# The state-space layer's GELU moved from the mix phase into the state-space units, and norms and bias rows issued sooner, in a hybrid state-space and attention block

## The chip, the cores and the metric

The kernel runs on one core of a Trainium2 chip. The metric is the time of one execution on the device in microseconds (us), and the median of several runs. Engines are named as in the profile: PE is TensorE (matmuls; PEld its weight loads), DVE is VectorE, ACT is ScalarE, POOL is GpSimd, SP is the engine whose queue issues nearly all DMA transfers (SPq).

## The reference

One layer over 2048 positions with model width 1024, all in 32-bit floats:

```python
proj = rmsnorm(x, norm_mix_g) @ w_in              # u (512), q, k, v (512 each)
# head group A: 32 groups of 16 channels, 64 complex states per group
_, states = lax.associative_scan(combine, (a, bu), axis=1)
y = einsum(states, c).real + d_skip * u
y = jax.nn.gelu(y)                                # the tanh form
y_ssm = y * jax.nn.sigmoid(y @ w_glu + b_glu)
# head group B: each 64-row chunk attends to itself and the 8 chunks before
probs = softmax(q k / 8 + relative_bias)
y_att = probs @ v                                 # 8 heads of 64
x = x + concat(rmsnorm(y_ssm), rmsnorm(y_att)) @ w_out
h2 = rmsnorm(x)
x = x + (silu(h2 @ w_gate) * (h2 @ w_up)) @ w_down
return rmsnorm(x)
```

## The kernel before

Products of 32-bit floats are made of three matmuls: each operand is split into a rounded high part (a cast on ScalarE) and a rest (a subtraction on VectorE), `split` at L153; names ending in h and l, or hi and lo, are such pairs.

The phases in order: a prologue (to about 145 us) with the state-space matrices and the state-space input u; the attention phase (to about 700 us); the mix phase (to about 960 us), which makes the GLU, the two norms and the output projection; gate and up; down.

The attention phase walks 128 steps, one for each query block of 512 rows (sb, four), head pair (pr), head (hh) and quarter (qp) of 128 queries. In a step `scores` makes the products of queries and keys (sc), adds the bias rows and takes the minimum in one VectorE instruction (mn<-sc,nba or nbb, L866), and ScalarE takes the exponential (L869). Two steps later `transp` transposes the row on TensorE (pt), and ScalarE and VectorE split it (pth L884, ptl L885). After a head's four steps `pv_head` multiplies by v (pj). The bias rows of a head are loaded by `load_nb` into one of two buffers (nba, nbb) while the head before is in work.

Beside the steps run generators called units. A `Unit` has a first and a last step, and at each step its generator goes on as far as its share asks; `pre` lets its first part, mostly loads, go earlier. `hT_unit` loads rows of x for the next query block (xt, raw), norms them (L744) and splits them (hi L745, lo L746). `qk_unit` and `v_unit` make the projections (pf). The state-space layer is eight blocks b of four groups: `ssm_front` loads U and multiplies by Bst, then scans on GpSimd; `ssm_back` multiplies by Tm and Vm, copies the result over U (L652) and stores it to the array y in memory (L654). Odd blocks and block 0 share one buffer U, the other even blocks the buffer rsn; X holds a block's states, XG the states shifted by one.

The tables SX and SY give the steps at which a block's front and back start; HTA and HTS those of the hT units, counted from the query block's first step. TensorE's instructions stay in the order in which the code emits them. Those of the other engines are ordered by a scheduler that goes by its own estimate of when operands and buffers are ready, so an instruction may stand far from its place in the code. Each engine then runs its queue strictly in order.

At step 119 (OPEN) the mix phase's first part becomes one more unit. `fetch` reads y back from memory into yr: for each partition 4 x 8 x 128 elements, in which neighbours in position stand 128 elements apart. `load` applies the GELU to yr with a gathering pattern into contiguous ys (L1050) and splits ys into gh and gl. `glu` multiplies by the GLU weights (wgh, wgl, whose raw rows come through two buffers sg) and multiplies ys by the sigmoid. For the first two blocks of 512 positions (late) the biased product goes into yr (L1077), one sigmoid covers all four quarters (L1079), and the products ys follow (L1081). Sums of squares (sq) give the norm's scale by Newton steps on VectorE (L98 to L110).

## Time and profile before

| | |
|---|---|
| median of 3 runs | 2264.99 us (2262.37 to 2267.28) |
| profiled execution: its own time | 2267.91 us |
| its span, mean granted TensorE clock | 2266.1 us, 0.982 |
| TensorE busy | 2165.6 us, 96% |
| VectorE, ScalarE, GpSimd busy | 1542.4, 1003.3, 351.2 us |
| TensorE busy in 650 to 700 and 700 to 750 us | 33.70 and 41.19 of 50 us |

The profile is one execution, so durations and gaps come from it, and its own time is what a sum of them is held against. In the rows of a timeline the first number is the start, the second the busy time, and the bracket at the end says how long the engine stood idle just before and which instruction ended it.

### The profile page before, as it was taken

What the parts mean: (1) busy time and instruction counts of PE and PEld (TensorE: products, weight loads), DVE (VectorE), ACT (ScalarE), POOL (GpSimd) and SP (SyncE); (2) the same over time, 40 slices, a digit from 0 to 9 for tenths busy, and PEclk for the clock granted to TensorE, in tenths of its full rate; (3) what the DMA queues carried; (4) which work ended last, traced back from release to release, by engine and by line L of the source; (5) the groups of instructions that cost most, each with busy time, mean ns of one, the idle gap of its engine ahead of it and who ended that gap; (6) DMA issues with size and microseconds to landing.
All of it is one profiled execution on the core that took longest, in us unless ns stands there. A gap on an engine that the chain in (4) does not pass through costs nothing.

```text
span 2266.1 us, 30134 instructions
## 1 busy us (share of the span) xinstructions
PE 2165.6 (96%) x10632; PEld 1825.8 (81%) x10632; DVE 1542.4 (68%) x2695; ACT 1003.3 (44%) x1656; POOL 351.2 (15%) x827
## 2 busy tenths in 40 slices
PE   8988899999997899999999999999999999999997
PEld 6777788898986788778888887888888778888886
DVE  7756666556557756776766668766656477688776
ACT  5445555556557442353333335333333443353322
POOL 2246576656500000000000000000000010000000
PEclk9999999999998899999999999999999999999999
DMA  8878876666552435754556457645433395465652
GB/s 276 254 244 261 268 233 207 192 190 205 187 168 100 138 109 188 251 168 144 180 176 209 162 198 269 199 163 190 140 97 112 102 385 182 167 227 181 216 183 75
DMA packets 194903, 430.41 MB, mean 190 GB/s; under 512 B 19904, under 2 KB 38384, under 8 KB 187648
## 3 DMA queue, kind: packets, MB, share of 16 engines
q1 hardware_dynamic: 187104, 403.58, 53.8%
q0 software_dynamic: 7648, 24.92, 3.6%
q8 instruction: 83, 1.36, 0.2%
q14 instruction: 68, 0.56, 0.1%
HBM read 288.95 MB, written 131.10 MB: 185 GB/s over the span
## 4 chain that ended last, share of the span: by engine, by line
PE 78%; DMA 7%; DVE 6%; ACT 3%; issue 2%; SPq 0%; DVEq 0%; ACTq 0%
PE X L76 20%; PE ps L76 17%; PE Y L76 10%; PE pf L76 10%; PE big L76 6%; PE W L76 5%; PE pj L76 4%; PE pt L79 2%; PE sc L76 2%; DMA acc<-x 2%; DMA lo<-hc 1%; DMA xt<-in_xt 1%; DVE lo L153 1%; DMA hc<-gh 1%; DVE ptl L885 1%
## 5 line engine op out<-in xcount | busy, mean ns | idle before, releaser
L76 PE MATMUL X<-hi,c 128*128 128x512 f32 x1408 | 450.8, 391 | 7.4 <-DVE c L153 5.1
L76 PE MATMUL ps<-hd,hd 128*128 128x512 f32 (+1 forms) x1968 | 429.6, 380 | 3.0 <-DVE hd L153 2.0
L76 PEld LDWEIGHTS ps<-hd,hd 128*128 128x128 f32 x1968 | 357.5, 189 | 73.6 <-DVE hd L153 2.7
L76 PEld LDWEIGHTS X<-hi,c 128*128 128x128 f32 x1408 | 265.1, 188 | 64.1 <-DVE c L153 6.0
L76 PE MATMUL X<-lo,c 128*128 128x512 f32 x704 | 274.6, 390 | 0.0
L153 ACT CAST hd<-hd 128x1536 fp32r<-128x1536 f32 (+1 forms) x106 | 147.5, 1394 | 232.5 <-DMA hd<-hq 170.9
L76 PE MATMUL Y<-hi,c 128*128 128x512 f32 x704 | 226.0, 392 | 3.8 <-DVE c L153 2.3
L153 DVE TENSOR_TENSOR hd<-hd 128x1536 fp32r<-128x1536 f32 (+1 forms) x106 | 174.1, 1644 | 36.2 <-ACT hd L153 35.8
L153 DVE TENSOR_TENSOR c<-S,c 128x512 fp32r<-128x512 f32 x176 | 121.0, 688 | 103.6 <-ACT c L153 103.3
L1516 POOL DMA_DIRECT2D hd<-hq x7 | 5.3, 755 | 1173.2 <-PE X L76 1161.5
L1408 ACT COPY u<-X 128x512 f32<-128x512 f32 x132 | 77.4, 587 | 199.9 <-PE X L76 199.9
L153 ACT CAST c<-S 128x512 fp32r<-128x512 f32 x176 | 109.5, 622 | 122.5 <-PE Y L76 63.8
L76 PE MATMUL big<-m,woh 128*128 128x512 f32 x512 | 162.6, 399 | 0.0
L76 PEld LDWEIGHTS Y<-hi,c 128*128 128x128 f32 x704 | 133.3, 189 | 32.4 <-DVE c L153 2.8
L1550 DVE TENSOR_TENSOR acc<-acc,ps 128x512 f32<-128x512 f32 x196 | 130.2, 682 | 41.6 <-PE ps L76 41.3
L76 PEld LDWEIGHTS X<-lo,c 128*128 128x128 f32 x704 | 132.6, 188 | 27.4
L76 PE MATMUL pf<-hi,w 128*128 128x512 f32 x416 | 149.1, 410 | 0.0
L153 ACT CAST c<-raw 128x512 fp32r<-128x512 f32 x132 | 82.2, 622 | 149.1 <-PE Y L76 69.1
L76 PE MATMUL Y<-lo,c 128*128 128x512 f32 x352 | 137.7, 391 | 0.0
L885 DVE TENSOR_TENSOR ptl<-pt,pth 128x640 fp32r<-128x640 f32 (+3 forms) x152 | 98.3, 647 | 56.1 <-ACT pth L884 54.7
L869 ACT ACTIVATE s<-s,mn 128x640 f32<-128x640 f32 (+4 forms) x128 | 98.0, 765 | 64.1 <-DVE mn L866 58.1
L884 ACT CAST pth<-pt 128x640 fp32r<-128x640 f32 (+3 forms) x152 | 83.8, 551 | 85.6 <-PE pt L79 80.9
(448 smaller groups left out, 4274.1 us busy)
## 6 DMA issues: line engine op xcount, KB each, us to landing
w<-wss SPq DMA_DIRECT2D x36, 1024.0 KB, 6.2
hq<-g SPq DMA_DIRECT2D x140, 256.0 KB, 2.1
hd<-hq SPq DMA_DIRECT2D x35, 768.0 KB, 4.4
hd<-wc SPq DMA_DIRECT2D x35, 768.0 KB, 6.0
raw<-in_w_gate SPq DMA_DIRECT2D x44, 512.0 KB, 3.7
raw<-in_w_up SPq DMA_DIRECT2D x44, 512.0 KB, 4.2
wc<-px SPq DMA_DIRECT2D x66, 256.0 KB, 3.1
wss<-w SPq DMA_DIRECT2D x12, 1024.0 KB, 6.5
```

The source lines that it names most:

```text
L76: return self.tc.keep_in_program_order(self.tc.nc.tensor.matmul(*a, **b))
L79: return self.tc.keep_in_program_order(self.tc.nc.tensor.transpose(*a, **b))
L153: return nc.scalar.copy(hi, raw), nc.vector.tensor_tensor(lo, raw, f32(hi), op=ALU.subtract)
L869: nc.scalar.activation(s[:, :nk], s[:, :nk], AF.Exp, bias=mn[:], scale=-1.0, accum_out=sums[sb, pr][:, hh, qp : qp + 1])
L884: nc.scalar.copy(pth[:, a:b, qp, :], pt[:, a:b, :])
L885: nc.vector.tensor_tensor(ptl[:, a:b, qp, :], pt[:, a:b, :], f32(pth[:, a:b, qp, :]), op=ALU.subtract)
L1408: nc.scalar.copy(u[:], ps[:])
L1516: (nc.gpsimd if aside else nc.sync).dma_start(f32(lo), src.rearrange("g p c -> p g c"))
L1550: V.tensor_tensor(a, a, ps[:], op=ALU.add)
```

## The change

The GELU is taken out of the mix phase. In `ssm_back` it is made by hand from half the result, u: Square and Tanh on ScalarE, two instructions on VectorE, with XG as the room for the intermediate; 0.5 goes into the copy, and the store to y, still one transfer for the block, comes two yields after the last product. `ssm_back` now spans five steps instead of two, and the fronts and backs of blocks 5 to 7 start one to three steps earlier. `glu` and `load` read yr directly, with the gathering pattern in the splits gh and gl and in the products ys; the late bias and sigmoid now work on contiguous ys. `hT_unit`'s second part is cut in two, norms first and splits later, and its loads and norms come four or more steps earlier; the bias rows are loaded at the second quarter of the head before instead of the third.

```diff
QS = 4, 5, 6, 7, 0, 1, 2, 3
-HTA = -12, -9
+HTA = -16, -13
 HTS = -8, -6
-HTP = 2
+HTN = -13, -8
 PRO = 0, 0, 2, 2, 2, 2, 0, 0, 0
...
 MAGIC = 12582912.0
+GELU = 0.044715
 F2 = NF // 2
...
         k.XG = k.t(p, "XG", [P, GB, NC])
-        nc.gpsimd.memset(k.XG[:, :, 0:1], 0.0)
     XG = k.XG
+    nc.gpsimd.memset(XG[:, :, 0:1], 0.0)
     XGv = XG[:].rearrange("p (q g) c -> p q g c", g=2)
...
             k.ta.matmul(ps[:, g2, :], vm[:, g, :], XG[:, g, :], start=False, stop=True)
-        nc.scalar.copy(U[:, 2 * q : 2 * q + 2, :], ps[:])
+        u, t = U[:, 2 * q : 2 * q + 2, :], XG[:, 2 * q : 2 * q + 2, :]
+        nc.scalar.activation(u, ps[:], AF.Copy, scale=0.5)
+        nc.scalar.activation(t, u, AF.Square)
         yield
+    for q in range(GP):
+        u, t = U[:, 2 * q : 2 * q + 2, :], XG[:, 2 * q : 2 * q + 2, :]
+        nc.vector.scalar_tensor_tensor(t, t, 0.25 / GELU, u, op0=ALU.add, op1=ALU.mult)
+        nc.scalar.activation(t, t, AF.Tanh, scale=8.0 * GELU * math.sqrt(2.0 / math.pi))
+        yield
+    for q in range(GP):
+        u, t = U[:, 2 * q : 2 * q + 2, :], XG[:, 2 * q : 2 * q + 2, :]
+        nc.vector.scalar_tensor_tensor(u, t, 1.0, u, op0=ALU.add, op1=ALU.mult)
+        yield
+    yield
+    yield
     nc.sync.dma_start(S["y"].rearrange("j (c g) t -> (j c) (g t)", c=CH)[:, GB * NC * b : GB * NC * (b + 1)], U.rearrange("p g t -> p (g t)"))
...
 SSM_F = 1 + GP + 7 + 7 + 3 + 4 + 1
-SSM_B = 1 + GP + 1
+SSM_B = 1 + 3 * GP + 3
 ST = 2, 10
-SX = 4, 24, 35, 48, 61, 74, 87, 100
-SY = 20, 36, 49, 62, 75, 88, 101, 114
+SX = 4, 24, 35, 48, 61, 73, 85, 97
+SY = 20, 36, 49, 62, 75, 87, 99, 111
...
+            def norm(q):
+                nc.vector.scalar_tensor_tensor(xts[q], xts[q], k.gm[:, q : q + 1], S["rsn"][:, ts], op0=ALU.mult, op1=ALU.mult)
+
...
                     load(q, 2)
+                for q in range(q0, q1):
+                    yield
+                    norm(q)
             for q in range(q0, q1):
                 yield
-                if q0 == 0 and q + 2 < q1:
-                    load(q + 2)
-                xt = xts[q]
+                if q0 == 0:
+                    if q + 2 < q1:
+                        load(q + 2)
+                    norm(q)
                 for v, n in zip(hT[sb], ("hi", "lo")):
                     v.append(k.t(aw, f"{n}{q}x" if q < DB and sb % 2 else f"{n}{q}", [P, SB], F32R)[:])
-                nc.vector.scalar_tensor_tensor(xt, xt, k.gm[:, q : q + 1], S["rsn"][:, ts], op0=ALU.mult, op1=ALU.mult)
-                nc.scalar.copy(hi[q], xt)
-                nc.vector.tensor_tensor(lo[q], xt, f32(hi[q]), op=ALU.subtract)
+                nc.scalar.copy(hi[q], xts[q])
+                nc.vector.tensor_tensor(lo[q], xts[q], f32(hi[q]), op=ALU.subtract)
             yield
...
             hd = st_head[sb, h]
-            if qp == 2 and (sb, h) < (NSB - 1, H - 1):
+            if qp == 1 and (sb, h) < (NSB - 1, H - 1):
                 nbs[(h + 1) % H] = load_nb((h + 1) % H)
...
         psum2 = cx.enter_context(tc.tile_pool(name="aps2", bufs=1, space=bass.MemoryType.PSUM, reuse_waits="tile"))
+        hts = {sb: hT_unit(sb, DB) for sb in range(1, NSB)}
         units = []
...
                     units.append(Unit(hT_unit(sb, 0, DB), 2 + DB, g0 + HTA[0], g0 + HTA[1], 2))
-                units += [Unit(hT_unit(sb, DB), 2 + KT - DB, g0 + HTS[0], g0 + HTS[1], HTP), Unit(qk_unit(sb, 0), QK_N, g0 + C[0], g0 + C[1], 3, light=LIGHT)]
+                units += [Unit(islice(hts[sb], 1 + KT - DB), 1 + KT - DB, g0 + HTN[0], g0 + HTN[1], 1), Unit(hts[sb], 1 + KT - DB, g0 + HTS[0], g0 + HTS[1]), Unit(qk_unit(sb, 0), QK_N, g0 + C[0], g0 + C[1], 3, light=LIGHT)]
             units.append(Unit(v_unit(sb, 0), V_N, g0 + C[1], g0 + C[2], 2, light=LIGHT) if sb else Unit(v0, V_N, *V0, done=1))
...
         for b in range(NG // GB):
-            units.append(Unit(ssm_front(k, sp, psum, S, b, k.ssm_eng), SSM_F, SX[b], SX[b] + 9, SX[b] - 2 if b == 0 else 2 if b == 1 else 5, light=SL))
-            units.append(Unit(ssm_back(k, sp, psum, S, b), SSM_B, SY[b], SY[b] + 2, 6, light=SL))
+            units.append(Unit(ssm_front(k, sp, psum, S, b, k.ssm_eng), SSM_F, SX[b], SX[b] + 9, SX[b] - 2 if b == 0 else 2 if b == 1 else 3, light=SL))
+            units.append(Unit(ssm_back(k, sp, psum, S, b), SSM_B, SY[b], SY[b] + 5, 6, light=SL))
         N = len(steps)
...
-        def load(sb, one=False):
+        def byt(a):
+            return a.rearrange("p (c j) -> p c j", j=L)
+
+        def load(sb):
             b = B()
             b.o = {}
-            yt = k.t(my, "ys", [P, 4, SB], bufs=2)
-            b.ys, b.g = [yt[:, f] for f in range(4)], []
+            b.yt = k.t(my, "ys", [P, 4, SB], bufs=2)
+            b.ys, b.g = [b.yt[:, f] for f in range(4)], []
             if sb and sb % 2 == 0:
                 fetch(sb)
-            yv = b.yr = yrs[0][:, :, :, (sb % 2) * 64 : (sb % 2 + 1) * 64]
-            fs = [slice(0, 4)] if one else [slice(f, f + 1) for f in range(4)]
-            for s in fs:
-                nc.scalar.activation(yt[:, s].rearrange("p f (c j) -> p f c j", j=L), yv[:, s].rearrange("p f j c -> p f c j"), AF.Gelu_apprx_tanh)
+            b.yr = yrs[0][:, :, :, (sb % 2) * 64 : (sb % 2 + 1) * 64].rearrange("p f j c -> p f c j")
             for f in range(4):
                 gh, gl = k.t(my, f"gh{f}", [P, SB], F32R), k.t(my, f"gl{f}", [P, SB], F32R)
-                split(k, gh[:], gl[:], b.ys[f])
+                split(k, byt(gh[:]), byt(gl[:]), b.yr[:, f])
                 b.g.append((gh, gl))
...
-
-            def by8(a):
-                return a.rearrange("p (a b) -> p a b", a=L)
...
                 if late:
-                    nc.vector.tensor_scalar(b.yr[:, f], by8(ps[:, :512]), bg[:, f : f + 1], None, op0=ALU.add)
+                    nc.vector.tensor_scalar(b.ys[f], ps[:, :512], bg[:, f : f + 1], None, op0=ALU.add)
                     if f == 3:
-                        nc.scalar.activation(b.yr, b.yr, AF.Sigmoid)
+                        nc.scalar.activation(b.yt[:], b.yt[:], AF.Sigmoid)
                         for i in range(4):
-                            nc.vector.tensor_tensor(by8(b.ys[i]), by8(b.ys[i]), b.yr[:, i], op=ALU.mult)
+                            nc.vector.tensor_tensor(byt(b.ys[i]), byt(b.ys[i]), b.yr[:, i], op=ALU.mult)
                 else:
...
                     nc.scalar.activation(sg[:], ps[:, :512], AF.Sigmoid, bias=bg[:, f : f + 1])
-                    nc.vector.tensor_tensor(b.ys[f], b.ys[f], sg[:], op=ALU.mult)
+                    nc.vector.tensor_tensor(byt(b.ys[f]), byt(sg[:]), b.yr[:, f], op=ALU.mult)
                 yield
...
         wr = rx.enter_context(tc.tile_pool(name="wr", reuse_waits="tile", bufs=2, side="right"))
-        b = load(0, True)
+        b = load(0)
         load_a(b, 0)
...
             yield
-        nxt = load(1, True)
+        nxt = load(1)
         for _ in range(PZ):
```

Three places where instructions stand otherwise; line numbers of the changed kernel are some 1 to 20 higher for the same operation.

ScalarE at the start of the mix phase: L869 (L889 after) is the exponential, s the softmax row, wgh a GLU weight's high part. Before:

```order
L869 ACTIVATE s_7962,sm_7946<-s_7962,mn_7963 128x640
L869 ACTIVATE s_7982,sm_7946<-s_7982,mn_7983 128x640
L1050 ACT_TABLE_LOAD
L1050 ACTIVATE ys_8026<-yr_7910 128x2048
L153 CAST wgh_1710_7915<-sg_7917 128x512
L153 CAST wgh_1713_7921<-sg_7923 128x512
L908 COPY yt_8007<-pj_7990 64x512
L884 CAST pth_8010<-pt_8012 128x5x128
L153 CAST gh_1742_8028<-ys_8026 128x512
L153 CAST gh_1744_8032<-ys_8026 128x512
L153 CAST gh_1746_8036<-ys_8026 128x512
```

After:

```order
L154 CAST gh_1742_8098<-yr_7981 128x512
L889 ACTIVATE s_8035,sm_8017<-s_8035,mn_8036 128x640
L904 CAST pth_7928<-pt_8039 128x5x128
L154 CAST gh_1744_8102<-yr_7981 128x512
L889 ACTIVATE s_8053,sm_8017<-s_8053,mn_8054 128x640
L154 CAST gh_1746_8106<-yr_7981 128x512
L154 CAST gh_1748_8110<-yr_7981 128x512
L154 CAST wgh_1710_7986<-sg_7988 128x512
L154 CAST wgh_1713_7992<-sg_7994 128x512
L928 COPY yt_8078<-pj_8061 64x512
L904 CAST pth_8081<-pt_8083 128x5x128
L1044 ACTIVATE sq_8122<-ya_1750_8114 128x512
```

Then one more cast wgh and the next exponential follow. The load of tables and the Gelu are gone, and the casts gh read yr and stand between exponentials.

SP's queue at the end of block 0: y<-U stores the block, U<-u reloads the buffer for block 1, xt and raw are rows for `hT_unit`, k<-ks loads keys. Before:

```order
L654 DMA y_65<-U_1708 128x1024
L788 DMA q2h_2507<-q2h_2507 64x512
L789 DMA q2l_2508<-q2l_2508 64x512
L788 DMA q2h_2510<-q2h_2510 64x512
L789 DMA q2l_2511<-q2l_2511 64x512
L711 DMA w_2618<-wss_74 128x2048
L726 DMA xt_2659<-in_xt 128x512
L726 DMA raw_2661<-in_xt 128x2x512
L726 DMA raw_2663<-in_xt 128x2x512
L566 DMA U_2665<-u_64 128x1024
L566 DMA Bst_2667<-bsts_70 128x512
```

After:

```order
L731 DMA wss_74<-w_2452 128x2048
L567 DMA Bst_2678<-bsts_70 128x512
L780 DMA k_597_2746<-ks_68 128x512
L668 DMA y_65<-U_1708 128x1024
L814 DMA ks_68<-k_547_2532 128x512
L814 DMA ks_68<-k_550_2535 128x512
L550 DMA nbb_1550<-nbs_69 64x576
L567 DMA U_2676<-u_64 128x1024
L551 DMA nbb_1550<-nbs_69 64x576
```

The rows of xt and raw now stand ahead of these; the store stands four places before the reload instead of nine, behind a load of k.

VectorE near the first query block's end, 640 columns a step from here on. L744 (L745 after) is the norm of a row of x, ptl the rest of the softmax split. Before:

```order
L866 ISA s_3269,mn_3270<-sc_3264,nba_107 128x640
L866 ISA mn_3270 128x1
L744 SCALAR_TENSOR_TENSOR raw_4423<-raw_4423,g_mix_87,rsn_93 128x512
L909 TENSOR_TENSOR ya_3024<-pj_3277,yt_3286 64x512
L744 SCALAR_TENSOR_TENSOR raw_4423<-raw_4423,g_mix_87,rsn_93 128x512
L885 TENSOR_TENSOR ptl_3290<-pt_3291,pth_3289 128x5x128
L744 SCALAR_TENSOR_TENSOR raw_4425<-raw_4425,g_mix_87,rsn_93 128x512
L866 ISA s_3322,mn_3323<-sc_3317,nba_107 128x640
L866 ISA mn_3323 128x1
L918 TENSOR_TENSOR ya_3024<-ya_3024,pj_3326 128x512
L744 SCALAR_TENSOR_TENSOR raw_4425<-raw_4425,g_mix_87,rsn_93 128x512
```

After, the norms of the same rows stand among the last steps of the query block before:

```order
L745 SCALAR_TENSOR_TENSOR raw_4221<-raw_4221,g_mix_87,rsn_93 128x512
L905 TENSOR_TENSOR ptl_2857<-pt_2944,pth_2856 128x2x128
L745 SCALAR_TENSOR_TENSOR raw_4223<-raw_4223,g_mix_87,rsn_93 128x512
L886 ISA s_2988,mn_2989<-sc_2985,nbb_1550 128x256
L886 ISA mn_2989 128x1
L905 TENSOR_TENSOR ptl_2857<-pt_2992,pth_2856 128x128
L745 SCALAR_TENSOR_TENSOR raw_4223<-raw_4223,g_mix_87,rsn_93 128x512
L905 TENSOR_TENSOR ptl_2857<-pt_2992,pth_2856 128x3x128
L886 ISA s_3028,mn_3029<-sc_3025,nbb_1550 128x384
L886 ISA mn_3029 128x1
```

And at the place where they stood:

```order
L886 ISA s_3168,mn_3169<-sc_3163,nba_107 128x640
L886 ISA mn_3169 128x1
L905 TENSOR_TENSOR ptl_3046<-pt_3173,pth_3045 128x128
L745 SCALAR_TENSOR_TENSOR xt_4048<-xt_4048,g_mix_87,rsn_93 128x512
L905 TENSOR_TENSOR ptl_3046<-pt_3173,pth_3045 128x2x128
L745 SCALAR_TENSOR_TENSOR xt_4219<-xt_4219,g_mix_87,rsn_93 128x512
L847 TENSOR_TENSOR v_676_3053<-pf_3181,v_676_3053 128x4x64
L886 ISA s_3233,mn_3234<-sc_3228,nba_107 128x640
L886 ISA mn_3234 128x1
L905 TENSOR_TENSOR ptl_3046<-pt_3237,pth_3045 128x128
```

The four norms of raw have moved ahead by more than 20 rows, and one or two of xt are left in their place.

## The prediction

> **What bounds the kernel now.** I read the page first, then TensorE's waits, then a table of stretches, and only then single instructions. The page's first part:
>
> ```profile
> PE 2165.6 (96%) x10632; PEld 1825.8 (81%) x10632; DVE 1542.4 (68%) x2695; ACT 1003.3 (44%) x1656; POOL 351.2 (15%) x827
> ```
>
> TensorE is busy for 96% of the span, and nothing in this change adds or removes a matmul. So the change moves the time only where TensorE stands still, and the question is how much of that standing still it touches. The table of stretches (columns: bounds, length, then busy time of TensorE, weight load, VectorE, ScalarE and GpSimd, TensorE's granted clock, DMA share, GB/s) says where it is:
>
> ```profile
> 450.00:650.00 200.00, 199.68 (x1270) 183.03 (x1269) 111.90 (x203) 115.16 (x230) 107.38 (x268) 1.00 0.61 186
> 650.00:700.00 50.00, 33.70 (x184) 28.68 (x183) 28.08 (x50) 36.74 (x53) 0.00 (x0) 0.86 0.53 163
> 700.00:750.00 50.00, 41.19 (x201) 33.58 (x201) 45.12 (x90) 35.56 (x50) 0.00 (x0) 0.90 0.41 134
> ```
>
> From 450 to 650 us, the later attention steps, TensorE never stops. From 650 to 750, where attention ends and the mix phase begins, it stands for 25.1 us of 100, and the granted clock falls to 0.86 and 0.90. Its waits say for whom it stands; first from 640 to 760 us, then in the earlier attention steps, 150 to 430 us (columns: us in total, times, longest):
>
> ```profile
> PE pt L79 <- DVE ptl L885: 13.8, 3, 6.4
> PE big L79 <- DVE no L110: 7.9, 1, 7.9
> ```
>
> ```profile
> PE pt L79 <- DVE ptl L885: 8.0, 7, 3.1
> PE sc L76 <- DVE mn L866: 5.8, 1, 5.8
> PE sc L76 <- DVE k L792: 4.1, 1, 4.1
> ```
>
> **Part 1: the GELU leaves the mix start.** The 13.8 us are three gaps in the last softmax steps. TensorE's next transposes (pt) wait for ptl, which waits for the cast pth; behind them the exponentials stand in ScalarE's queue. ScalarE's timeline shows what lies between two exponentials:
>
> ```profile
> 675.15 1.28 ACT L1050 ACT_TABLE_LOAD   x1 [0.30 <-DMA yr<-y]
> 676.45 3.69 ACT L1050 ACTIVATE ys<-yr 128x2048 f32<-128x2048 f32 x1
> ...
> 684.47 0.61 ACT L153 CAST wgh<-sg 128x512 fp32r<-128x512 f32 x1
> ...
> 686.67 1.28 ACT L869 ACT_TABLE_LOAD   x1
> 687.97 0.83 ACT L869 ACTIVATE s<-s,mn 128x640 f32<-128x640 f32 x1
> ...
> 691.33 1.28 ACT L1050 ACT_TABLE_LOAD   x1
> 692.62 3.80 ACT L1050 ACTIVATE ys<-yr 128x2048 f32<-128x2048 f32 x1
> ```
>
> Out go two Gelus (3.69 + 3.80 = 7.5 us) and these three loads of tables (3 x 1.28 = 3.8 us): 11.3 us. Some is paid back, since the casts gh now read the stored rows through a stride. What a stride costs is in these groups (busy us, mean ns):
>
> ```profile
> L1050 ACT ACTIVATE ys<-yr 128x512 f32<-128x512 f32 x8 | 8.7, 1124 | 2.3 <-DVE m L153 2.3
> ...
> L153 ACT CAST gh<-ys 128x512 fp32r<-128x512 f32 x16 | 9.0, 619 | 1.7 <-PE pf L76 1.6
> ...
> L478 ACT COPY rsn<-pb 128x512 f32<-128x512 f32 x3 | 3.4, 1148 | 0.1
> ```
>
> A Gelu of 512 elements, gathering every 128th word, took 1.12 us, a plain copy with a stride (L478) 1.15, a cast of contiguous rows 0.62. So the Gelu's price is that of its gathering, and I price a gathering cast at 1.12 us instead of 0.62. Four of them cost 2.0 us here: the chain gains at most 11.3 - 2.0 = 9.3 us. The Trainium skill, "Advanced Engine Details and Errata", section "Memory Cachelines", has it as a rule: accesses that fall into another 16-byte line each time pay a penalty. The rows above agree, and by that rule the removed Gelu's price comes back in whatever reads the rows next.
>
> The lower bound: in the changed order the cast wgh at 684.47 still stands ahead of the first exponential (687.97). If its weight row comes no sooner, that exponential gains 687.97 - 685.08 = 2.9 us, and the second gap may gain nothing. Between 2.9 and 9.3 I take **-7**: 2.9 at the first, and 4.1 of the 5.1 us of load and Gelu at 691.33, since two squares that stood behind the exponential now stand before it.
>
> The same stride costs VectorE, where the differences gl and the products ys (L1081) go from contiguous to gathered operands:
>
> ```profile
> L153 DVE TENSOR_TENSOR gl<-ys,gh 128x512 fp32r<-128x512 f32 x16 | 10.0, 685 | 4.2 <-ACT gh L153 4.2
> ...
> L1081 DVE TENSOR_TENSOR ys<-ys,yr 128x512 f32<-128x512 f32 x8 | 5.2, 685 | 0.5 <-ACT yr L1079 0.4
> ...
> L483 DVE TENSOR_TENSOR us<-ps,rsn 128x512 f32<-128x512 f32 x4 | 4.3, 1120 | 0.5 <-ACT rsn L473 0.5
> ```
>
> Four gl and all eight products lie between 700 and 750 us, where VectorE is nearly full (45.12 of 50) and TensorE ends by waiting 7.9 us for VectorE's Newton steps (L110). Nothing hides them. L483 is the nearest row, a two-operand instruction with one gathered operand: 12 x (1.120 - 0.685) = **+5.2**, between 0 and 5.2. The clock: 33.70 us at 0.86 hold 33.70 x 0.14 = 4.7 us of slowness that follows the pauses. With 7 of 16.3 us of pauses gone there, I take **-2** (0 to -3). The Gelus of blocks two and three lie beside a TensorE that the page shows full: nothing, and were that cover gone, 8 x 0.5 us either way.
>
> **Part 2: the GELU enters the state-space units.** Each of 8 blocks has two halves; each half gets a Square and a Tanh on ScalarE and two instructions of the kind scalar-tensor-tensor on VectorE. The nearest rows:
>
> ```profile
> L652 ACT COPY U<-pj 128x512 f32<-128x512 f32 x10 | 5.9, 586 | 8.5 <-PE pj L76 8.5
> ```
>
> ```profile
> L1098 DVE SCALAR_TENSOR_TENSOR ys<-ys,gs,big 128x512 f32<-128x512 f32 x16 | 11.0, 742 | 0.0
> ```
>
> That is 16 x 2 x 0.59 = 18.9 us on ScalarE and 16 x 2 x 0.742 = 23.7 us on VectorE. From 450 to 650 they are busy 115 and 112 of 200 us beside a full TensorE, which covers them: 0 there, and rival (b) if not. No load of tables stands between exponentials in the changed order. The Trainium skill ("ScalarE activation tables: per-element evaluation and per-set limits", the opening steps) says that two functions in one set need no switch; no run shown here tells whether Exp and Tanh are such a pair.
>
> Cover is thin at block 0. The store of its rows, the reload of the same buffer for block 1, and TensorE's wait after it:
>
> ```profile
> 228.42 0.33 SPq L654 DMA_DIRECT2D y<-U  x1
> ...
> 236.61 0.71 SPq L566 DMA_DIRECT2D U<-u  x1
> ```
>
> ```profile
> 245.65 3.35 PE L76 MATMUL pj<-U,Bst 128*128 128x256 f32 x8 [4.04 <-DMA Bst<-bsts]
> ```
>
> ```profile
> U<-u SPq DMA_DIRECT2D x1, 512.0 KB, 8.3
> ```
>
> ```profile
> y<-U SPq DMA_DIRECT2D x1, 512.0 KB, 3.7
> ```
>
> In the changed order four VectorE products (3.0 us), four norms moved ahead of them (3.0) and ScalarE's second Square and Tanh (1.2) stand before the store: 228.4 + 7.2 = 235.6, and up to 237 with the k load that it now follows on SP. The reload waits for the store to land. A transfer of this size landed in 8.3 us here and in 3.7 where the queues were light (the second row): the reload lands between 235.6 + 7.4 = 243.0 and 237 + 16.6 = 253.6, against the present 245.65: -2.7 to +8, and I take **+2**. Behind the waiting reload on SP stand the second half of a bias row and the next units' weights and rows, which come later by as much. VectorE's added work ahead of ptl in that stretch: **+1** (0 to +4).
>
> **Part 3: norms and bias rows sooner.** At the borders of the query blocks VectorE's norms and differences stand ahead of what TensorE waits for:
>
> ```profile
> 284.89 2.14 DVE L744 SCALAR_TENSOR_TENSOR raw<-raw,g_mix,rsn 128x512 f32<-128x512 f32 x1
> ```
>
> ```profile
> 381.49 2.99 DVE L746 TENSOR_TENSOR lo<-raw,hi 128x512 fp32r<-128x512 f32 x2
> ```
>
> The first stands, with another norm, before the ptl of the 3.1 us gap. In the changed order the four norms are more than 20 rows earlier on VectorE: that gap goes, **-3** (0 to -3.1; VectorE waits in order for their rows, whose transfers now fall where the queues are full). The second stands before the k of the 4.1 us gap; there the changed order is the same row for row: 0. The bias rows come one step sooner. The 5.8 us gap behind the bias minimum (mn) has the splits of the projection weights on the same queue; the minimum now comes ahead of them, and TensorE meets the splits next: 0 (-1 to +2).
>
> **The sum**, against the profiled execution's 2267.91 us (span 2266.1): -7 + 5.2 - 2 + 2 + 1 - 3 = -3.8. The profiled execution lies 2.9 us above the median of 2264.99, which I take off: **2261** as a median.
>
> **The rivals.** (a) *The gain becomes a new wait at the mix start*: the first exponential moves by 2.9 only, held by the weight row behind which it stands, the second gap and the clock gain nothing, the strided work is whole: -2.9 + 5.2 + 0 = +2.3, 2267. For it: VectorE at 45.12 of 50. Against: a load and a Gelu leave the second gap as well. (b) *Slower: the GELU is not covered inside attention.* Both queues run in order, so an exponential waits behind Tanh, a ptl behind the products. The price is what a half adds to VectorE, 1.5 us, wherever it reaches TensorE: 16 halves make 24 us, half of them 12, and the sum is then -3.8 + 12 = +8.2: 2273; with the reload at its upper end 6 more, 2279. It decides from 0.5 us a half (8 us) upward. For it: single bursts of 2 to 3 us did reach TensorE at the borders. Against: 450 to 650 shows no wait. (c) *Better*: a gathered operand costs VectorE nothing in these two forms, and the chain gains its whole 9.3: -9.3 + 0 - 3 - 2.7 + 0 - 3 = -18: 2247. For it: L483's other operand lies in PSUM, those of gl and ys do not. Against: ScalarE's price for the same rows.
>
> **How the numbers follow.** Forecast 0.44, (a) 0.10, (b) 0.24, (c) 0.22. A difference of 0.2%, 4.5 us, is about what a measurement of this kernel can tell from none, so the line lies at 2260.5 and my forecast beside it. Its own spread (2251 to 2268) gives 0.26 faster, 0.14 same, 0.04 slower; (c) 0.22 faster; (a) 0.04 same, 0.06 slower; (b) 0.02 and 0.22. Together 0.48, 0.20, 0.32. The range 2245 to 2274 leaves out the farther half of (b) and the farther end of (c).
>
> **What would show it.** Right: no Gelu and three loads of tables in all; the three gaps of 13.8 us at 6 to 8; gl and the products ys at about 1.1 us on VectorE; the wait for the Newton steps longer than 7.9; the 3.1 us gap gone and the 4.1 us gap still there. Wrong: gl and ys at 0.69 us; a wait for U<-u of more than 8 us; waits for ptl or mn scattered over 300 to 650 us, where TensorE now has next to none.

## The result and the profile after

The changed kernel took 2274.41 us (median of 6 runs, 2271.40 to 2281.65) beside 2263.02 us for the kernel before on the same chip: a ratio of 1.005, 95% interval 1.0037 to 1.0062, slower by 11.4 us. The forecast was 2261. The time is the one that the prediction gave for rival (b).

The page of the profiled execution (2274.28 us, span 2272.5, mean granted clock 0.980), its line of busy times:

```profile
PE 2172.2 (96%) x10632; PEld 1830.1 (81%) x10632; DVE 1574.6 (69%) x2727; ACT 995.7 (44%) x1666; POOL 365.4 (16%) x834
```

The same matmuls; 32 more instructions on VectorE. Next the stretches of the prediction, columns as there:

```profile
450.00:650.00 200.00, 197.11 (x1235) 178.91 (x1234) 121.89 (x215) 121.32 (x241) 121.77 (x280) 1.00 0.59 182
650.00:700.00 50.00, 41.11 (x233) 35.60 (x232) 33.83 (x57) 31.30 (x58) 0.00 (x0) 0.91 0.61 196
700.00:750.00 50.00, 42.02 (x209) 34.68 (x207) 43.27 (x76) 32.04 (x41) 0.00 (x0) 0.94 0.28 100
```

The mix start is better filled (41.11 for 33.70, clock 0.91 for 0.86), but from 450 to 650, where TensorE was full with 199.68, it now stands for 2.9 us of 200. TensorE's waits, from 640 to 760 us and from 150 to 430 us:

```profile
PE big L80 <- DVE no L111: 7.9, 1, 7.9
PE pt L80 <- DVE ptl L905: 4.8, 2, 3.9
PE big L77 <- DVE ya L938: 3.0, 1, 3.0
```

```profile
PE pj L77 <- ACT X L585: 7.2, 2, 6.4
PE pt L80 <- DVE ptl L905: 5.2, 5, 1.9
PE sc L77 <- DVE mn L886: 4.2, 2, 3.3
PE sc L77 <- DVE k L812: 3.1, 1, 3.1
```

The wait for ptl at the mix start is 4.8 instead of 13.8, and a wait of 6.4 us for X, the states' buffer, is new in attention. Since every stretch shifts the next one, I compared the starts of the same TensorE instructions: the first product with Bst, the 14th and the last of the 16 groups pj<-ident,rb (one for each query block and head pair), and the second and eighth groups pf/big<-ident,no, the Newton steps' results. The kernel before was profiled a second time for this, as before_again, since its first profile had lain 2.9 us above its median. Lengths in us:

| stretch | before | before_again | after | after less each |
|---|---|---|---|---|
| start to first Bst | 160.69 | 160.92 | 159.56 | -1.1, -1.4 |
| attention, to the 14th rb | 486.54 | 481.55 | 497.47 | **+10.9, +15.9** |
| mix start, to the last rb | 72.06 | 74.93 | 65.94 | **-6.1, -9.0** |
| to the second no (first Newton steps in the way) | 26.54 | 26.25 | 30.68 | **+4.1, +4.4** |
| later mix, to the eighth no | 188.18 | 187.87 | 192.12 | **+3.9, +4.2** |
| to the end | 1332.09 | 1329.48 | 1326.73 | -5.4, -2.8 |
| span | 2266.1 | 2261.0 | 2272.5 | +6.4, +11.5 |

Both columns tell one story: the mix start gains what was forecast, the gathered operands take back about what was forecast, and attention loses eleven to sixteen where +3 (Part 2) and -3 (Part 3), together nothing, were forecast. The last row belongs to code that the change does not touch; among all profiles of this document it lies between 1326.7 and 1332.1, so it is spread between executions.

The attention row can be cut further, at the fifth and the ninth group pj<-ident,rb. Each entry is the length, and in brackets how long TensorE was busy in it; the numbers of matmuls are the same within two:

| part of attention | before | before_again | after |
|---|---|---|---|
| first part, first Bst to the 5th rb | 166.26 (146.40) | 162.35 (144.69) | 174.72 (149.40) |
| middle part, to the 9th rb | 147.36 (140.58) | 146.28 (140.34) | 146.22 (141.95) |
| last part, to the 14th rb | 172.92 (172.79) | 172.92 (172.79) | 176.53 (173.82) |

So the loss lies in the first part (+8.5 or +12.4), where block 0 is stored and its buffer reloaded, and in the last one (+3.6), which the forecast had at 0. Of the 10.9 or 15.9 in all, TensorE stands still for 5.5 or 8.5 of them; the other 5.4 or 7.4 is the same matmuls taking longer, at a mean granted clock of 0.97 instead of 0.98. The length of the last part is worth keeping: it repeats within 0.1 us from profile to profile, while that of the first part differs by 3.9 between two profiles of one kernel.

### The profile page after: what moved, and what is told of

It reads as the page before. It is cut to its first block, busy times and chain, and to the rows that moved or that the text cites. A ratio compares the mean times of both kernels' runs of the same rounds, so it can differ in the third digit from the quotient of the medians.

```text
span 2272.5 us, 30175 instructions
## 1 busy us (share of the span) xinstructions
PE 2172.2 (96%) x10632; PEld 1830.1 (81%) x10632; DVE 1574.6 (69%) x2727; ACT 995.7 (44%) x1666; POOL 365.4 (16%) x834
## 4 chain that ended last, share of the span: by engine, by line
PE 77%; DVE 7%; DMA 5%; issue 3%; ACT 3%; POOL 2%; SPq 0%; DVEq 0%; ACTq 0%; POOLq 0%
PE X L77 20%; PE ps L77 18%; PE Y L77 10%; PE pf L77 10%; PE big L77 6%; PE W L77 5%; PE pj L77 4%; PE pt L80 2%; PE sc L77 2%; DMA lo<-hc 1%; DMA hd<-wc 1%; DMA x<-xt 1%; DVE lo L154 1%; DVE ptl L905 1%; DMA yr<-x 0%
## 5 line engine op out<-in xcount | busy, mean ns | idle before, releaser
L889 ACT ACTIVATE s<-s,mn 128x640 f32<-128x640 f32 (+4 forms) x128 | 97.8, 764 | 66.2 <-DVE mn L886 61.3
```

The lines of the kernel that those rows point to most:

```text
L889: nc.scalar.activation(s[:, :nk], s[:, :nk], AF.Exp, bias=mn[:], scale=-1.0, accum_out=sums[sb, pr][:, hh, qp : qp + 1])
```

## The experiments

A ratio is always to the kernel before, run on the same chip at the same time.

**Which half of the change.** rows_only is the kernel before with Part 3 alone: the edits to HTA, HTN and `hT_unit`, and `qp == 1`. gelu_only is the changed kernel with these undone.

> The kernel before with part 3 alone (norms and bias rows sooner; the GELU stays in the mix phase). If the loss comes from the GELU inside the state-space units: within 3 us of the kernel before, on the faster side if the 3.1 us gap at the first border goes. If it comes from the norms, which now run beside GpSimd's scan of block 1 and stretch it: 3 to 7 us slower than before, with GpSimd's scan of block 1 at about 42 us instead of 39.

> The changed kernel with part 3 undone (norms and bias rows where they were before). If the GELU in the units is the cause: 2272 to 2276 us, and TensorE's wait behind the X copies of block 2 stays at 4 us or more. If the moved norms are the cause: 2265 to 2269 us, that wait under 1 us, GpSimd's scan of block 1 back at 39 us.

rows_only: 2266.26, ratio 1.0016 (1.0007 to 1.0025). gelu_only: 2274.52, 1.0052 (1.0040 to 1.0064). The GELU's move alone loses all that the change loses, and Part 3 alone gains nothing. But rows_only does not test what Part 3 was to do at the 3.1 us gap. VectorE's timeline ahead of it, and TensorE's at it, first in rows_only:

```profile
284.49 2.15 DVE L731 SCALAR_TENSOR_TENSOR raw<-raw,g_mix,rsn 128x512 f32<-128x512 f32 x1
```

```profile
289.04 1.33 PE L79 MATMUL pt<-ident,s 128*128 128x128 f32 x5 [3.13 <-DVE ptl L891]
```

Then in before_again:

```profile
284.18 0.74 DVE L744 SCALAR_TENSOR_TENSOR raw<-raw,g_mix,rsn 128x512 f32<-128x512 f32 x1
```

```profile
287.26 0.76 PE L79 MATMUL pt<-ident,s 128*128 128x128 f32 x5 [1.66 <-DVE ptl L885]
```

In rows_only the scheduler left the four norms of raw where they stood in the kernel before, in spite of the edit, and the gap is there as before. In before_again the first of these norms takes 0.74 us instead of 2.15, and the gap is shorter by about as much: the norm ahead of ptl does set it. In the changed kernel the last of these norms ends at 268 us, and the transposes at the same place (289.20) start without a wait in the profile. They do so in gelu_only too (291.61), whose code has Part 3 undone but whose norms of raw the scheduler also put ahead, to 263 to 266 us.

**The visible wait, and the late products.** The wait for X comes about like this in the changed kernel. ScalarE, and TensorE behind it:

```profile
302.40 3.02 ACT L585 COPY X<-pj 64x256 f32<-64x256 f32 x8 [11.07 <-DMA XG<-X]
```

```profile
303.95 1.22 PE L77 MATMUL pj<-U,Tm 128*128 128x256 f32 x2 [6.39 <-ACT X L585]
```

The copies into X may not begin before the last transfer out of X has been read, and ScalarE, which runs in order, stands behind the first of them for 11 us. The front of block 2 two steps later, and the late products ys on GpSimd instead of VectorE:

```diff
-SX = 4, 24, 35, 48, 61, 73, 85, 97
+SX = 4, 24, 37, 48, 61, 73, 85, 97     # front2_later
...
-nc.vector.tensor_tensor(byt(b.ys[i]), byt(b.ys[i]), b.yr[:, i], op=ALU.mult)
+nc.gpsimd.tensor_tensor(byt(b.ys[i]), byt(b.ys[i]), b.yr[:, i], op=ALU.mult)   # late_products_pool
```

> The changed kernel with one number altered: block 2's front starts at step 37 instead of 35, so that its copies into X no longer meet the transfer that still reads X. If ScalarE's 11 us standstill there costs TensorE its 6.4 us gap and the slow clock behind it: 4 to 6 us faster than the changed kernel, about 2269, with that gap gone. If scan follows scan so closely that the wait only moves to block 3: no change, 2274, with a new wait for X near 355 us.

> The changed kernel with the eight late products ys on GpSimd instead of VectorE. If VectorE's gathered work is what TensorE waits for before the Newton steps: 8.2 us of VectorE work gone from 716 to 753 us, the 7.9 us wait down to 3 or less, 4 to 6 us faster than the changed kernel. If the products then take longer in series (a GpSimd operation on 434 columns took 1.06 us, so about 1.25 us each) and the squares wait for them: 0 to 2 us slower.

front2_later: 2272.30, 1.0039 (1.0027 to 1.0051). late_products_pool: 2274.47, 1.0055 (1.0041 to 1.0069). In front2_later the 6.4 us wait is gone, yet only some 2 us come back, which the intervals do not tell from none; another wait stands near its place (there is no new wait for X near 355 us):

```profile
298.09 0.82 PE L80 MATMUL pt<-ident,s 128*128 128x128 f32 x5 [2.35 <-DVE ptl L905]
```

And late_products_pool, with the attention code of the changed kernel, shows only 1.6 us of that wait at the longest and is no faster; gelu_only shows 1.6 too, where its text expected 4 or more, and takes the full time:

```profile
PE pj L77 <- ACT X L585: 2.4, 2, 1.6
```

So the most visible wait of the trace is not the cause: kernels as slow do without it. GpSimd took the late products one behind the other, and the wait for the Newton steps grew:

```profile
PE big L80 <- DVE no L111: 12.2, 1, 12.2
```

**The two halves of the GELU's move, each done otherwise.** gelu_direct keeps the mix phase of the changed kernel, but makes the GELU in the state-space units with the Gelu function, as it copies out of PSUM, and stores where the kernel before did; the starts and the norms too are those of the kernel before. gather_on_pool is the changed kernel with a mix phase in which GpSimd's copies do the gathering into ys, so that ScalarE and VectorE read contiguous rows as before. direct_and_pool does both in the kernel before. old_starts is the changed kernel with SX and SY of before.

```diff
-        nc.scalar.copy(U[:, 2 * q : 2 * q + 2, :], ps[:])
+        nc.scalar.activation(U[:, 2 * q : 2 * q + 2, :], ps[:], AF.Gelu_apprx_tanh)   # gelu_direct
...
-                nc.scalar.activation(yt[:, s] ..., yv[:, s] ..., AF.Gelu_apprx_tanh)
+            for f in range(4):                                                        # gather_on_pool
+                nc.gpsimd.tensor_copy(yt[:, f].rearrange("p (c j) -> p c j", j=L), yv[:, f].rearrange("p j c -> p c j"))
```

> Attention phase as in the kernel before, but the copy of a block's result (L652) applies the Gelu table function itself: 16 loads of tables (20.5 us of ScalarE, about what Square and Tanh cost), nothing on VectorE, no later store. Mix phase as in the changed kernel. If the loss inside attention comes from the two VectorE instructions of each half and the later store: the attention phase loses at most 3 us to the kernel before, 2264 to 2267 us in all. If it comes from ScalarE's added time in an ordered queue, whatever fills it: 2272 us or more.

> The changed kernel with the gathering done by copies on GpSimd, which is idle in the mix phase: ys is copied contiguous, and the casts gh, the differences gl and the products ys work on contiguous rows as in the kernel before; yr is read by nothing after the copies. If the gathering operands cost what the rows said (gl and ys 1.07 to 1.10 us instead of 0.69, gh 1.11 instead of 0.62) and the buffer yr is held too long for the rows of x that follow: 5 to 10 us faster than the changed kernel, 2265 to 2269. If the copies are late (1.2 us each, four in a row ahead of the first cast) or slow VectorE down: no change.

> Both of these edits together. If both reasons hold: 8 to 16 us faster than the changed kernel, 2258 to 2266, at or below the kernel before. If either turns into a new wait: 2268 or more.

> The changed kernel with the starts of the fronts and backs of blocks 5 to 7 as before (74, 87, 100 and 88, 101, 114). If the earlier starts cause the small stalls of 450 to 650 us (3.8 us in all): 3 to 4 us faster than the changed kernel. If the GELU's own instructions do: no change there, and the last block's store comes later, 0 to 3 us slower at the mix start.

| kernel | median, us | ratio |
|---|---|---|
| gelu_direct | 2264.47 | 1.0004 (0.9993 to 1.0015) |
| gather_on_pool | 2266.10 | 1.0014 (1.0001 to 1.0027) |
| direct_and_pool | **2256.34** | **0.9971 (0.9961 to 0.9980)** |
| old_starts | 2272.96 | 1.0045 (1.0029 to 1.0061) |

Each of the first two replacements takes back 8 to 10 us, and both together beat both kernels: 7.3 us under the kernel before. old_starts lies between its two theories, and its interval does not tell it from the changed kernel. The price of one gathering instruction was right. In the changed kernel (groups by line):

```profile
L154 ACT CAST gh<-yr 128x512 fp32r<-128x512 f32 x16 | 17.4, 1113 | 2.7 <-DMA yr<-y 1.6 <-PE pf L77 1.1
L154 DVE TENSOR_TENSOR gl<-yr,gh 128x512 fp32r<-128x512 f32 x16 | 16.7, 1088 | 1.5 <-ACT gh L154 1.5
...
L1098 DVE TENSOR_TENSOR ys<-ys,yr 128x512 f32<-128x512 f32 x8 | 8.2, 1068 | 0.1
```

In direct_and_pool the gathering stands on an engine that has nothing else to do there, and ScalarE's table goes back and forth eight times:

```profile
L652 ACT ACT_TABLE_LOAD x8 | 10.3, 1283 | 0.1
...
L869 ACT ACT_TABLE_LOAD x8 | 10.3, 1283 | 1.9 <-DVE mn L866 1.8
...
L1050 POOL COPY ys<-yr 128x512 f32<-128x512 f32 x16 | 20.0, 1299 | 145.6 <-DVE m L153 102.9 <-DVE rs L895 42.7
```

Those 16 loads of 1.28 us, which a GELU by hand would avoid, stand between exponentials of attention and cost no time that the medians can tell. In the trace the eight of them that fall into the last part of attention show a little: it takes 174.11 to 174.14 us in gelu_direct, direct_and_pool and direct_late_store instead of 172.92. There the loads have cover, at the mix start they had none.

gather_on_pool shows one more thing. In the changed kernel yr is read up to the last product ys, so rows of x that are loaded into the same buffer come later, and VectorE waits in order for them with Newton steps behind. VectorE and TensorE in the changed kernel, then the same TensorE group in gather_on_pool:

```profile
888.14 0.75 DVE L1336 SCALAR_TENSOR_TENSOR yr<-yr,g_ffn,rsn 128x512 f32<-128x512 f32 x1 [2.13 <-DMA yr<-x]
```

```profile
896.14 1.76 PE L77 MATMUL big<-ones,sq 128*128 128x1 f32 x8 [2.36 <-DVE nv L103]
```

```profile
893.37 1.05 PE L77 MATMUL big<-ones,sq 128*128 128x1 f32 x8 [0.25 <-DVE nv L103]
```

That is part of the later mix's +3.9 to +4.2; in gather_on_pool that stretch is 188.0, as before, and the one ahead of it 26.9. The size is one execution's: old_starts, with the same mix code as the changed kernel, takes 188.7 for the later mix, while the +4 of the stretch ahead of it comes back in all kernels with gathered operands (30.7 to 32.4, or 34.6 with the late products on GpSimd).

**Store, products, chain.** What in the hand-made GELU costs the time, if its table loads do not? Starting from gelu_direct, direct_late_store moves only the store, to where the changed kernel has it; direct_two_reads keeps the store and puts two products of the changed kernel's kind on VectorE for each half, on XG, whose results nobody uses; direct_one_read puts one reduction over XG there.

```diff
+    for _ in range(2 * GP + 2):      # direct_late_store; SSM_B and the ends of the backs as in the changed kernel
+        yield
     nc.sync.dma_start(S["y"] ...
...
+    nc.vector.scalar_tensor_tensor(t, t, 1.0, t, op0=ALU.add, op1=ALU.mult)      # direct_two_reads, twice for each half
```

> The kernel gelu_direct with the back spread over five steps and the store to y as late as in the changed kernel (nothing on VectorE still). If the late store and the reload behind it make the loss inside attention: 4 to 8 us slower than gelu_direct, 2268 to 2272, with block 1's scan on GpSimd at 42 to 43 us and a wait behind the X copies of block 2. If VectorE's added instructions make it: within 2 us of gelu_direct, 2263 to 2266, TensorE at block 1's first product waiting 2 to 5 us for the reload but nothing after it.

> The kernel gelu_direct with the two VectorE instructions of each half added behind the store, as idle work on XG that nothing waits for (both operands in SBUF, as in the changed kernel; 32 of them, 24 us). If these instructions by themselves make the larger part of the loss inside attention: 3 to 7 us slower than gelu_direct, 2268 to 2271, and GpSimd's scans 1 to 3 us longer each. If the loss came from the chain Square, product, Tanh, product that the store waits for: within 1.5 us of gelu_direct.

> The same with a sum over the same 512 columns in place of each added instruction: one operand in SBUF instead of two. If VectorE and GpSimd get in each other's way at the second SBUF operand: scans as in gelu_direct (38.5 us for the later blocks) and a time within 1.5 us of it, below direct_two_reads. If the added time on VectorE counts, whatever it reads: the same as direct_two_reads.

> The kernel before once more, for a second profile of it. No theory parts here: its TensorE landmarks should lie within 1 to 2 us of those of the first profile up to 650 us, since kernels that share that code do.

direct_late_store: 2267.57, 1.0013 (1.0004 to 1.0022), between its two theories. direct_two_reads: 2263.33, 1.0001 (0.9991 to 1.0010). before_again: 2262.98 in one run; its 14th rb group starts at 642.47 instead of 647.23, so that one kernel's profiles differ by 4.8 us there and not by the 1 to 2 that were expected. direct_one_read: 2457.93, and it says nothing on its question: its reductions were queued ahead of other work and VectorE stood behind transfers into XG, as its waits show (us in total, times, longest):

```profile
DVE dm L658 <- DMA XG<-X: 194.6, 8, 25.6
```

The 32 products, 1.5 us a half, cost nothing on their own, although VectorE and ScalarE are as busy in direct_two_reads as in the changed kernel: 311.5 and 293.9 us within attention, against 309.5 and 291.8. GpSimd's scans are stretched too (busy for 297.5 us, 302.6 in the changed kernel, 288.4 before), and that is free as well. Four more kernels build up what lies between 2267.6 and 2274.5. late_and_products is direct_late_store with the two products. units_old_starts is gelu_only with the starts of before, so that only the way in which a half is worked out separates it from late_and_products. split_chains has the instructions of units_old_starts in the same rows, but ScalarE's three work on U and VectorE's two on XG, so that neither engine waits for the other; no_first_product is the changed kernel without the first product, so that Tanh waits for nothing of VectorE's. The last two give other values for the state-space layer.

```diff
-        nc.scalar.activation(t, u, AF.Square)                                            # split_chains
+        nc.scalar.activation(u, u, AF.Square)
-        nc.vector.scalar_tensor_tensor(t, t, 0.25 / GELU, u, op0=ALU.add, op1=ALU.mult)  # no_first_product: this line out
+        nc.vector.scalar_tensor_tensor(t, t, 0.25 / GELU, t, op0=ALU.add, op1=ALU.mult)
-        nc.scalar.activation(t, t, AF.Tanh, ...)
+        nc.scalar.activation(u, u, AF.Tanh, ...)
-        nc.vector.scalar_tensor_tensor(u, t, 1.0, u, op0=ALU.add, op1=ALU.mult)
+        nc.vector.scalar_tensor_tensor(t, t, 1.0, t, op0=ALU.add, op1=ALU.mult)
```

> The Gelu straight from PSUM with its table load, the store of a block late as in the changed kernel, and per half the two scalar-tensor-tensor products on VectorE at the rows where the changed kernel has them, but no instruction of ScalarE waits for them; the products overwrite XG, which nothing reads any more. The late store alone measured 2267.6, the products alone 2263.3. Theory A (the rest of the loss is the chain Square, product, Tanh, product, in which ScalarE waits in order for VectorE): 2267 to 2269, the two parts simply add. Theory B (late store and products are each harmless but take each other's slack, block 1's scan being stretched to 43 us while its X buffers are still held): 2271 to 2275, and a wait of TensorE for X of over 4 us near 304 us.

> The changed kernel without the first product of the hand-made GELU: Tanh reads the square, so ScalarE never waits for VectorE between Square and Tanh; one VectorE instruction of 0.78 us less in each half, and the values of the state-space layer are other than the reference's. The changed kernel measured 2274.4. Theory A (the chain across two in-order queues): 2268 to 2270, most of the loss in attention goes with the link. Theory B (VectorE's volume beside the scan, and the late store): the volume falls by half, the store stays late: 2271 to 2273, and the wait for X near 304 us stays at over 3 us.

> The kernel before with the GELU in the units and the mix phase of the changed kernel, but the units' starts and the norms and bias rows where they were before: beside late_and_products (2270.8) it differs only in how a half is worked out: Copy, Square and Tanh on ScalarE and the two products linked to them, in place of one Gelu with its table loads and two free products. Theory A (what is left of the loss is the linked chain and ScalarE's added instructions): 2273 to 2275, as with the new starts (2274.5). Theory B (it is the earlier starts): 2270 to 2272.

> units_old_starts with the same instructions in the same rows, but ScalarE's three work on U alone and VectorE's two on XG alone, so that neither engine waits for the other between Copy and store; the values of the state-space layer are other than the reference's. Theory A1 (the link between two in-order queues costs): 2270 to 2271.5, the time of late_and_products. Theory A2 (the number of instructions in the two queues costs, linked or not): the time of units_old_starts, within 1.5 us.

The whole ladder, with the lengths of the first and the last part of attention in each profile (166.26 or 162.35 and 172.92 before):

| kernel | what is added | median, us | ratio | first part, us | last part, us |
|---|---|---|---|---|---|
| gelu_direct | Gelu out of PSUM, 16 table loads | 2264.47 | 1.0004 (0.9993 to 1.0015) | 164.83 | 174.11 |
| direct_two_reads | two free products a half, store early | 2263.33 | 1.0001 (0.9991 to 1.0010) | 164.00 | 174.34 |
| direct_late_store | store late, no products | 2267.57 | 1.0013 (1.0004 to 1.0022) | 169.22 | 174.12 |
| late_and_products | store late, two free products a half | 2270.84 | 1.0024 (1.0012 to 1.0036) | 170.20 | 174.35 |
| split_chains | Copy, Square, Tanh, unlinked | 2268.60 | 1.0022 (1.0011 to 1.0034) | 172.11 | 173.27 |
| units_old_starts | the links between the queues | 2272.68 | 1.0044 (1.0027 to 1.0060) | 173.96 | 175.14 |
| gelu_only | earlier starts | 2274.52 | 1.0052 (1.0040 to 1.0064) | 173.99 | 176.53 |
| changed kernel | norms and bias rows sooner | 2274.41 | 1.0050 (1.0037 to 1.0062) | 174.72 | 176.53 |

The intervals seldom separate neighbours. They do separate direct_two_reads from late_and_products, which differ in whether the block is stored ahead of the free products or behind them and two yields more: the late store costs 0.2%. It costs it in the first part, 4.4 and 6.2 us in the two pairs of kernels with an early and a late store, and nothing in the last. All six profiles with the store as before take 162.4 to 168.0 us for the first part, all eleven with the late store 169.2 to 174.9. TensorE's wait for the reload that follows the store of block 0 appears with it, here in direct_late_store and in late_and_products; in gelu_direct no such wait shows:

```profile
244.80 1.99 PE L76 MATMUL pj<-U,Bst 128*128 128x256 f32 x8 [0.57 <-DMA U<-u]
```

```profile
247.38 3.78 PE L76 MATMUL pj<-U,Bst 128*128 128x256 f32 x8 [5.63 <-DMA U<-u]
```

The 0.57 shows that this wait is not all of the 4.4; the rest is spread over other waits and a lower clock.

The intervals also separate late_and_products and split_chains from gelu_only, which has the links and the earlier starts. How these two divide, the last part tells, since it repeats so well:

- 172.92 to 172.94 in three profiles with the GELU in the mix phase (before, before_again, rows_only);
- 173.27 in split_chains, with all instructions of the hand-made GELU and no links;
- 175.14 in units_old_starts and again in old_starts, with the links: **+1.9**;
- 176.53 to 176.59 in the five kernels with the links and the earlier starts: **+1.4**;
- 174.93 in no_first_product, which has the earlier starts and one link less: 1.6 of it come back.

That makes the +3.6 of this part, in which the forecast had 0. The same instructions cost 0.35 us there without links, and the place of the store makes no difference there (174.34 and 174.35). In the first part the links cannot be told from the spread: the five kernels with the changed kernel's units and starts take 169.5 to 174.9. So theory A1 of split_chains came out in direction, in the ratio and in the last part (its median lies 1.4 below its range). On the medians the links are not resolved: split_chains and units_old_starts, on one chip in one batch, lie 4.1 us apart, but their intervals overlap between 1.0027 and 1.0034. late_and_products and units_old_starts measured between their two theories, and no_first_product, at 2274.22 or 1.0039 (1.0025 to 1.0053), lies outside the ranges of both of its own.

## Why the prediction was wrong

It was wrong in sign; the time lies just outside the range. By its own steps:

**Part 1, the mix start** (-7 and -2 for the clock): -6.1 against the first profile of before, -9.0 against the second. Right, and for the reason given: three table loads in all are left, and the waits for ptl fell from 13.8 to 4.8. The Trainium skill ("ScalarE activation tables: per-element evaluation and per-set limits", in the section "What a function is on this engine", the opening steps) says that two functions in one set need no switch. The trace shows Exp and Tanh to be such a pair: they alternate in attention, and none of the three loads (L439, L1096, L1468) stands there.

**Gathered operands** (+5.2): +4.1 to +4.4, with gl at 1088 ns and the products at 1068 to 1098, where 1120 was taken. Rival (c) was wrong on VectorE. The sign of it was foreseen as a longer wait for the Newton steps; that stayed at 7.9, and a wait of 3.0 for ya came on the way there.

**"The Gelus of blocks two and three: nothing"**: wrong, by +3.9 to +4.2 in this profile. I looked at the cover of the instructions and not at the buffer. yr used to be free after the Gelu and is now held up to the products, and what is loaded next into it comes late.

**Part 2, 0 in 450 to 650 and +3 for block 0** is the step that failed. In the last part of attention the 0 became +3.6, 1.9 for the links and 1.4 for the earlier starts. In the first part the late store alone, priced at +2 for the reload, cost 4.4 to 6.2, and the whole part lost 8.5 or 12.4. That the group after the reload starts at 247.71 instead of 245.65, just the +2 that was taken, is luck: in before_again it starts at 243.61, and TensorE waits less at this place than the 4.04 of the kernel before, since it arrives later.

```profile
247.71 3.68 PE L77 MATMUL pj<-U,Bst 128*128 128x256 f32 x8 [2.21 <-DMA U<-u]
```

I took "busy 115 and 112 of 200 us beside a full TensorE" as cover. It is cover for volume, and volume was not the cost: direct_two_reads, with the volume, costs nothing. What is not covered is order: a store that keeps its buffer longer, and steps that pass from one in-order queue to the other and back, behind each of which an exponential or a ptl can stand. The sum also had no term for the clock in attention, where the same matmuls took 5.4 or 7.4 us longer.

**Part 3, -3 for the 3.1 us gap**: the reading of the gap was right, and the gap is gone in the changed kernel. Its size was one execution's (1.66 in before_again), and the edits that were to remove it bought no time: gelu_only, without them, has no gap there either and takes the time of the changed kernel, and rows_only, with them alone, is 0.16% slower. That the 4.1 us gap stays (3.1 now) and the 5.8 us gap turns into other waits was right: the wait for mn is 3.3, those for the projection weights' splits 2.7 and 1.0 follow.

```profile
PE pf L77 <- ACT w L154: 2.7, 1, 2.7
...
PE pf L77 <- DVE w L154: 1.0, 1, 1.0
```

**Rival (b)** gave the time, 2273, and the sign that would show it, waits for ptl and others scattered over 300 to 650 us (1.8 us for ptl from 450 to 650, where there were none). That the time fits is luck in part. Its mechanism, exponentials behind Tanh and ptl behind products, fits the links, which show 1.9 us in the last part; its price, "what a half adds to VectorE, 1.5 us, wherever it reaches TensorE", does not hold, for the free products cost nothing; and the late store and the clock, which bring the rest, are not its mechanism. It had 0.24: the profile showed TensorE full for those 200 us, and I read that as slack of the others.

**What stays open**: what the links cost in the first part of attention, where executions of like kernels differ by 5 us; which single waits make up the late store's 4.4 to 6.2; and why the stretch after the mix phase differs by up to 5 us between profiles.

## What to carry to other kernels

Where the bound engine is full and the others are half idle, added work on them is cheap only if nobody waits for it: ask of each added instruction which in-order queue stands behind it, how many times the chain crosses from engine to engine, and how much longer it holds the buffer that the next transfer needs. And check in the trace that an edit moved what it was to move: a scheduler can leave it where it was. A table load or a special function that looks dear at a bare place can cost next to nothing where there is cover, so move the work as it stands before replacing it by a chain of cheap steps. Where profiles of one kernel differ by several us, look for a stretch that repeats, and compare there. A gathering read costs on whichever engine does it, so give it to the one that is idle there.

## What the runs showed of the hardware

I had not expected that 16 table loads of 1283 ns put between the exponentials of attention cost so little: 1.2 us for the eight in the last part of attention (174.11 for 172.92), and nothing that the medians tell (gelu_direct, 1.0004). GpSimd gathers 128 x 512 elements in 1.30 us, against 1.11 for ScalarE's cast with the same gathering: one engine's idle time bought back the price on the two that TensorE waits for. It was not quite free: while GpSimd does the gathering, the differences gl on contiguous rows take a mean of 837 ns in direct_and_pool and 879 in gather_on_pool, instead of 685 in the kernel before. Why is not tested.
